# Gate and up products of eight blocks: two of eight pairs of k tiles by seven block products

## The chip, the core and the metric

The kernel runs on one core of a Trainium2 chip. The metric is the device time of one execution in microseconds; the time before is the median of three runs. TensorE (PE in the profile) multiplies, VectorE (DVE), ScalarE (ACT) and GpSimd (POOL) work elementwise, SyncE (SP) issues most of the loads.

## The reference

One layer on 256 tokens of width 2048: a first gated feed-forward network (FFN) of width 5632, a mixer (an RWKV-7 scan and a pooling branch), and a second FFN, each between two norms and added to the residual. All is fp32. The change touches the two FFNs:

```python
def _swiglu(x, w_gate, w_up, w_down):
    return (jax.nn.silu(x @ w_gate) * (x @ w_up)) @ w_down

f = _swiglu(_rmsnorm(h, ln_ffn1_pre[l]), ffn1_gate[l], ffn1_up[l], ffn1_down[l])
h = h + MACARON_WEIGHT * _rmsnorm(f, ln_ffn1_post[l])
```

## The kernel before

Every fp32 product is made of three matmuls: each operand is split into a rounded high part H and a rest L, and H·H, H·L and L·H are added up in PSUM (`mm3`). For weights the split is done on the way: SyncE loads a tile of two k tiles by 512 columns (512 KB, buffer `w32`, 4 of them), ScalarE casts it to `wH`, VectorE subtracts to get `wL` (`two`; 5 buffers each of `wH` and `wL`). So each weight tile passes SyncE, ScalarE, VectorE and TensorE in turn. A buffer is free again when its last reader is done: a `w32` after `wL` is made, a `wH` and `wL` after the tile's last matmul.

`ffn` works through 11 blocks of 512 hidden columns. In a block `gemm_tok` makes the gate product, 16 k tiles by two halves h of 128 tokens, into two PSUM banks, then the up product. The norm of the input isn't applied to the inputs `uT` but to the products: `ev_g` and `ev_u` multiply by the row factor `rs[h]`, a scalar of each token. `ev_g` makes silu, `ev_u` multiplies and turns the block in 32 by 32 pieces into `T1` (`turn`, VectorE). `shuffle_split` then puts the pieces in place with 16 ScalarE copies of 32 partitions each into `x32`, casts them to H (ScalarE) and subtracts (VectorE): two of the tiles `hT` that the down product reads. It was called at the end of the block it belongs to.

The down product is made by `post` and `seven`, two column ranges of 512 at once. There six pairs of k tiles (`NQ`) are taken out of the plain sum: the pair of k tiles, the two token halves and the two column ranges make a 2 by 2 by 2 product of blocks, and `quad` makes it with seven block products in place of eight (Winograd's form). It needs sums of inputs (`sums`: `sx`, four `sf`, `sH`, `sL`; one call serves two quads) and sums of weights: `t13` and `t24`, made by VectorE from two `w32` buffers loaded by four 256 KB transfers. A quad splits 3.5 weight tiles where two plain pairs split 2. The products go to eight PSUM banks, and `merge` and `finish` add them up. In which place of the sequence of pairs a quad stands is listed in `QUADS`.

In which order the instructions stand in each engine's queue is decided when the program is built, by a scheduler that keeps its own estimate of times; code under `high_priority` (weight splits, evictions) goes ahead of other code. Only the beginnings and ends of the products with `lead` and `trail` are ordered by hand. Each engine then works its queue strictly in order: an instruction that waits holds up all behind it.

Lines that the prediction's steps name: 134 and 135 (cast and subtraction of a weight tile), 158 to 160 (the three matmuls), 218 to 231 (`sums`), 279 to 294 (`quad`: loads, `t13`, `t24`, splits), 322 to 331 (`merge`, `finish`), 466 (transposes), 483 (`turn`), 493 to 497 (`shuffle_split`), 512 to 518 (gate and up evictions).

Of the kernel before, what the change touches and what calls it, by code (L numbers as in the profile page):

```python
# [54 lines left out]
class Block:  # L55
    def __init__(s, tc, ctx):
        s.tc = tc
        s.nc = nc = tc.nc
        E = ctx.enter_context
        s.n = 0  # L60
        s.late, s.after, s.items, s.events, s.now = [], [], deque(), [], 0.0
        s.cp = E(tc.tile_pool(name="cp", bufs=1))
# [99 lines left out]
    def gemm_tok(s, w, c0, at, KT, evac, lead=False, trail=False, xs=None):  # L162
# [71 lines left out]

    def seven(s, w, cf, cl, at, KT, T, sm, ev_first, ev_last, trail):


        nc = s.nc
        V = nc.vector
        n = NQ  # L240
        K0 = 2 * n
# [18 lines left out]
        ws = {}  # L260

        def keep(tiles):
            ws.update((k, (wH, wL)) for k, wH, wL in tiles)

        def pair(k, c0, b):
            keep(s.load_w(w, k, 2, c0, 512))
            for i in range(2):
                for h in range(2):
                    mul(f"{b}{h}", rows(k + i, h), ws[k + i])

        def quad(q):
            k = 2 * q
            if len(sm) < min(q + 2, n):
                s.sums(T, sm)
            va, vb = [s.wp.tile([P, 1024], F32, tag="w32", name=s.nm("w32"), bufs=W32_BUFS)
                      .rearrange("p (a c) -> p a c", a=2) for _ in range(2)]
            for dst, kk, c0 in ((va[:, 0], k, cl), (vb[:, 0], k, cf), (va[:, 1], k + 1, cf),
                                (vb[:, 1], k + 1, cl)):
                nc.sync.dma_start(out=dst, in_=w[kk * P:kk * P + P, c0:c0 + 512])
# [40 lines left out]
        def merge():  # L320
            with s.tc.high_priority(offset=BOOST):
                nc.scalar.copy(u[0], bank["p1"])
                for o, b, i in ((1, "p6", 0), (2, "p7", 1), (3, "p5", 2), (1, "p5", 1),
                                (1, "f0", 1), (3, "f1", 3)):
                    V.tensor_tensor(out=u[o], in0=bank[b], in1=u[i], op=ALU.add)
                ev_first(0, u[1])
                ev_first(1, u[3])

# [4 lines left out]
        for i, k in enumerate(tiles):  # L333
            pair(k, cl, "l")
            if i in QUADS[trail][1]:
# [8 lines left out]
        s.now = 0.0  # L344
        s.by_half(w, cl, stop, KT, 0.0, AHEAD[0],
                  lambda k, h: mul(f"l{h}", rows(k, h), ws[k]), keep, finish)
# [155 lines left out]
    def ffn(s, wg, wu, wd, uT, rs, gpost, resid, emit, reload, xs=None):  # L502
        nc = s.nc
        hT = s.new_T(NKF // 4)
        at = s.T_at(uT)
        for b in range(NKF // 4):
            sig = [None, None]
# [9 lines left out]
            def ev_u(h, ps):  # L517
# [10 lines left out]
        s.post(wd, s.T_at(hT), NKF, gpost, 0.5, resid, emit, reload, hT)  # L528

    def post(s, wd, at, KT, gpost, fac, resid, emit, reload, hT=None):  # L530
        nc = s.nc
# [51 lines left out]
        if hT:  # L583
            sm = []
            for c in (0, 2):
                s.seven(wd, c * 512, c * 512 + 512, at, KT, hT, sm, ev_of(c), ev_of(c + 1),
                        c == 2)
            return
# [98 lines left out]
    def mixer(s, prm, uT, rs, resid, emit, gpost, reload):  # L687
# [13 lines left out]

        for h in range(2):
            t = s.tmp("rb")
            nc.vector.tensor_copy(t[:, :P], rs[h].to_broadcast([P, P]))
            ps = s.psum("rb")
            nc.tensor.transpose(ps[:, :P], t[:, :P], s.ident)
            nc.scalar.copy(s.rsb[:, h * P:h * P + P], ps[:, :P])

# [645 lines left out]
```

## Time and profile before

| | |
|---|---|
| median of 3 runs | 2091.64 us (2089.87 to 2092.41) |
| the profiled execution | 2090.64 us, of which the span from the first to the last instruction is 2088.9 us |
| TensorE's mean granted clock | 0.998 of full speed |
| TensorE, VectorE, ScalarE busy in one gate/up block of 43.52 us | 43.52, 24.34, 25.11 us |
| the same in 175 us of the first down product | 175.00, 143.39, 94.92 us |
| HBM | 194 GB/s over the span |

How to read the rows that follow. In the order of time a row is: start, duration, engine, line, operation, what it writes and reads, how many, and in brackets how long the engine idled before it and for whom. In the table by stretches it is: the stretch, its length, then the busy time of TensorE's matmuls, its weight loads, VectorE, ScalarE and GpSimd with the number of instructions, the granted TensorE clock, the share of the DMA engines and GB/s. In the groups by line it is: line, engine, operation, shapes, count, then busy us and mean ns, then idle us before and its releaser. A row of waits is: who waited for whom, us in total, times, longest. Matmuls are pipelined: they start about 0.227 us apart and each lasts 0.39 us in the records.

### The profile page before, as it was taken

Reading aid. Unit: us, or ns where it says so; the run is one execution under the profiler, and the core shown is the slowest. Engines: PE = TensorE matmul, PEld = TensorE weight load, DVE = VectorE, ACT = ScalarE, POOL = GpSimd, SP = SyncE. Lnnn points to the kernel's source line nnn. Section 1 sums busy time; section 2 is a strip of 40 time slices with the busy share of each in tenths; the row PEclk is TensorE's granted clock in tenths of the full one; section 3 lists DMA queues with packets and bytes.
Section 4 is the critical chain, followed back from the end, with each engine's and each line's share of the span. In section 5 each row is a group of like instructions: output and inputs, shape, how many; then the busy total and the mean of one; then the engine's idle time right before and its main releaser. Section 6 shows DMA issues by size and latency. Waiting matters only on the chain.

```text
span 2088.9 us, 29095 instructions
## 1 busy us (share of the span) xinstructions
PE 2072.3 (99%) x11017; PEld 1745.5 (84%) x11017; DVE 1387.7 (66%) x1776; ACT 1156.1 (55%) x1658; POOL 76.0 (4%) x161
## 2 busy tenths in 40 slices
PE   9999999999999999999999999999999999999998
PEld 7888888887888899999888788888888888878886
DVE  6555555556887765799688666575555555568876
ACT  6565555655555565474465444466655566555543
POOL 0000000000000010000110110010000000000000
PEclk9999999999999999999999999999999999999999
DMA  7656666565767766656456565566566666646674
GB/s 256 194 176 211 193 194 194 176 211 154 226 200 252 219 190 187 178 166 193 132 159 193 157 247 190 197 219 192 182 202 196 196 192 181 203 162 220 201 242 161
DMA packets 224885, 406.99 MB, mean 195 GB/s; under 512 B 13919, under 2 KB 49897, under 8 KB 224745
## 3 DMA queue, kind: packets, MB, share of 16 engines
q1 hardware_dynamic: 218569, 384.69, 59.8%
q0 software_dynamic: 5888, 19.93, 2.7%
q8 instruction: 86, 1.41, 0.3%
q10 hardware_dynamic: 288, 0.52, 0.1%
q14 instruction: 54, 0.44, 0.1%
HBM read 396.69 MB, written 8.39 MB: 194 GB/s over the span
## 4 chain that ended last, share of the span: by engine, by line
PE 95%; DVE 2%; issue 2%; ACT 1%; POOL 0%; DMA 0%; POOLq 0%; DVEq 0%; ACTq 0%
PE mm L158 26%; PE mm L159 26%; PE mm L160 26%; PE mc L438 10%; PE ms L159 1%; PE ms L160 1%; PE ms L158 1%; PE tr L466 1%; ACT x L493 1%; PE pA L1075 0%; DVE wL L135 0%; DVE wL L294 0%; PE pSa L1183 0%; DMA x<-in_x_dram 0%; DVE sx L218 0%
## 5 line engine op out<-in xcount | busy, mean ns | idle before, releaser
L135 DVE TENSOR_TENSOR wL<-w,wH 128x1024 fp32r<-128x1024 f32 (+2 forms) x677 | 810.6, 1209 | 552.2 <-ACT wH L134 549.0
L134 ACT CAST wH<-w 128x1024 fp32r<-128x1024 f32 (+2 forms) x677 | 698.0, 1044 | 625.5 <-PE mm L160 464.9
L159 PE MATMUL mm<-wL,xH 128*128 128x512 f32 x2316 | 902.2, 390 | 0.5 <-DVE wL L135 0.5
L160 PE MATMUL mm<-wH,xL 128*128 128x512 f32 x2316 | 902.2, 390 | 0.0
L158 PE MATMUL mm<-wH,xH 128*128 128x512 f32 x2316 | 896.5, 391 | 0.0
L160 PEld LDWEIGHTS mm<-wH,xL 128*128 128x128 f32 x2316 | 435.0, 188 | 91.6 <-DVE xL L474 0.8
L158 PEld LDWEIGHTS mm<-wH,xH 128*128 128x128 f32 x2316 | 435.2, 188 | 90.3
L159 PEld LDWEIGHTS mm<-wL,xH 128*128 128x128 f32 x2316 | 435.3, 188 | 89.9 <-DVE wL L135 1.3
L438 PE MATMUL mc<-xH,wH 128*128 128x256 f32 x560 | 159.5, 285 | 0.0
L438 PE MATMUL mc<-xL,wH 128*128 128x256 f32 x560 | 158.4, 283 | 0.0
L438 PE MATMUL mc<-xH,wL 128*128 128x256 f32 x560 | 158.3, 283 | 0.0
L493 ACT COPY x<-T 32x256 f32<-32x256 f32 x352 | 141.9, 403 | 3.9
L438 PEld LDWEIGHTS mc<-xH,wH 128*128 128x128 f32 x560 | 106.0, 189 | 1.1
L438 PEld LDWEIGHTS mc<-xH,wL 128*128 128x128 f32 x560 | 106.0, 189 | 0.2
L438 PEld LDWEIGHTS mc<-xL,wH 128*128 128x128 f32 x560 | 106.0, 189 | 0.1
L293 ACT CAST wH<-t 128x1024 fp32r<-128x1024 f32 x48 | 50.5, 1053 | 64.2 <-DVE t L286 47.9
L293 ACT CAST wH<-w 128x1024 fp32r<-128x1024 f32 (+1 forms) x48 | 40.0, 838 | 58.8 <-DMA w<-in_ffn_down_dram 48.3
L294 DVE TENSOR_TENSOR wL<-t,wH 128x1024 fp32r<-128x1024 f32 x48 | 58.6, 1221 | 20.9 <-ACT wH L293 20.8
L547 POOL DMA_DIRECT2D gb<-in_ln_ffn_post_dram x4 | 2.4, 592 | 1215.1 <-DVE wL L294 1215.1
L283 DVE TENSOR_TENSOR t<-w,w 128x1024 f32<-128x1024 f32 x24 | 29.4, 1224 | 23.7 <-DMA w<-in_ffn_down_dram 22.1
L294 DVE TENSOR_TENSOR wL<-w,wH 128x1024 fp32r<-128x1024 f32 (+1 forms) x48 | 44.2, 952 | 0.7 <-ACT wH L293 0.6
L512 ACT ACTIVATE sg<-mm,rs 128x512 f32<-128x512 f32 x44 | 29.9, 689 | 22.3 <-PE mm L160 22.3
(284 smaller groups left out, 1502.9 us busy)
## 6 DMA issues: line engine op xcount, KB each, us to landing
w<-in_ffn_up_dram SPq DMA_DIRECT2D x176, 512.0 KB
w<-in_ffn_gate_dram SPq DMA_DIRECT2D x174, 512.0 KB
w<-in_ffn_down_dram SPq DMA_DIRECT2D x128, 512.0 KB
w<-in_w_in_dram SPq DMA_DIRECT2D x128, 512.0 KB
w<-in_ffn_down_dram SPq DMA_DIRECT2D x96, 256.0 KB
w<-in_w_out_dram SPq DMA_DIRECT2D x32, 512.0 KB
w<-in_w_proj_b_dram SPq DMA_DIRECT2D x16, 512.0 KB
w<-in_w_proj_a_dram SPq DMA_DIRECT2D x16, 512.0 KB
```

Of the source, the lines that this page charges most:

```text
L134: s.nc.scalar.copy(vH, v)
L135: s.nc.vector.tensor_tensor(out=vL, in0=v, in1=vH.bitcast(F32), op=ALU.subtract)
L158: nc.tensor.matmul(ps, aH, bH, start=start, stop=False)
L159: nc.tensor.matmul(ps, aH, bL, start=False, stop=False)
L160: nc.tensor.matmul(ps, aL, bH, start=False, stop=stop)
L283: V.tensor_tensor(out=t13, in0=va, in1=vb[:, :1].to_broadcast([P, 2, 512]), op=ALU.subtract)
L293: nc.scalar.copy(H, v)
L294: V.tensor_tensor(out=L, in0=v, in1=H.bitcast(F32), op=ALU.subtract)
L438: s.nc.tensor.matmul(o, lh, rh, start=one and n == 0, stop=k == KT - 1 and n == 2, skip_group_check=True)
L466: nc.tensor.transpose(ps[:, i], src[:, i * P:(i + 1) * P], s.ident)
L493: nc.scalar.copy(dst[q * 32:q * 32 + 32, :, :, i], src[i * 32:i * 32 + 32, :, :, q])
L512: nc.scalar.activation(out=sg, in_=ps, func=AF.Sigmoid, scale=rs[h])
```

## The change

Blocks 2 to 9 of each FFN (`FAST`) make the gate and up product in one call of `seven`: the gate's 512 columns are its first range, the up's 512 its second, and two pairs of k tiles (k 0 to 3) are quads. The first quad stands after the fourth pair of the gate (of six), the second after the second pair of the up product. The sums of inputs must hold the normed input, so `normed` builds it once per FFN at the end of block 0: `spread` lays the row factor out along the free axis (two transposes), and each of four `uT` tiles is put together, multiplied by it, and split again into `nT` (three VectorE operations and one cast each). One call of `sums` on `nT` serves all eight blocks. Blocks 0 and 1 are made as before, block 10 as before but on `nT` with a factor of 1.

In the new evictions `ev_f` lets ScalarE write the sigmoid into a PSUM bank that is free (`p1` or `p6`) and multiplies, `ev_l` multiplies and turns.

The carrying of a block's `T1` into `hT` (the 16 copies and the split) is put off: it is entered into the list `soft`, and `soften` empties it in the middle of the next product (in `gemm_tok` at k tile 8, in `seven` at its fifth pair). The tiles of `hT` are made then and not at the beginning. The first sum for the down product is made in block 10 between gate and up, and later ones two pairs after a quad, in place of ahead of it.

```diff
+FAST = range(2, 10)
@@ gemm_tok
             for k2 in range(k0, k1, 4):
+                if k2 == 8:
+                    s.soften()
@@
-    def seven(s, w, cf, cl, at, KT, T, sm, ev_first, ev_last, trail):
+    def seven(s, wf, cf, wl, cl, at, KT, T, sm, n, spots, ev_first, ev_last, trail=False):
...
-        n = NQ
         K0 = 2 * n
...
-        def pair(k, c0, b):
+        def pair(k, w, c0, b):
             keep(s.load_w(w, k, 2, c0, 512))
+            since[0] += 1
+            if since[0] == 2 and len(sm) == n - left["p1"] < n:
+                s.sums(T, sm)
...
         def quad(q):
             k = 2 * q
-            if len(sm) < min(q + 2, n):
-                s.sums(T, sm)
...
             mul("l1", rows(k + 1, 1), t4)
-
-        if not sm:
-            s.sums(T, sm)
+            since[0] = 0
+
...
         for i, k in enumerate(range(K0, KT, 2)):
-            pair(k, cf, "f")
-            if i in QUADS[trail][0]:
+            pair(k, wf, cf, "f")
+            if i == 4:
+                s.soften()
+            if i in spots[0]:
                 quad(next(q))
...
-                ev_first(0, u[1])
-                ev_first(1, u[3])
+                ev_first(0, u[1], bank["p1"])
+                ev_first(1, u[3], bank["p6"])
@@ ffn
-        hT = s.new_T(NKF // 4)
+        hT, sm = [], []
...
+        def carry(T1, b):
+            hT.extend(s.new_T(1))
+            s.shuffle_split(T1, hT, b)
...
-                    s.shuffle_split(T1, hT, b)
-
+                    s.soft.append(lambda T1=T1, b=b: carry(T1, b))
+
+            def ev_f(h, u, free):
+                nc.scalar.activation(out=free, in_=u, func=AF.Sigmoid)
+                nc.vector.tensor_tensor(out=u, in0=u, in1=free, op=ALU.mult)
+                sig[h] = u
+
+            def ev_l(h, o):
+                nc.vector.tensor_tensor(out=o, in0=o, in1=sig[h], op=ALU.mult)
+                s.turn(T1, h, o)
+                if h == 1:
+                    s.soft.append(lambda T1=T1, b=b: carry(T1, b))
+
+            if b in FAST:
+                s.seven(wg, b * 512, wu, b * 512, s.T_at(nT), NKD, nT, su, 2, ((3,), (1,)),
+                        ev_f, ev_l)
+                continue
+            if b > 1:
+                rs = [1.0, 1.0]
+                at = s.T_at(nT)
             s.gemm_tok(wg, b * 512, at, NKD, ev_g, lead=(b == 0), xs=xs if b == 0 else None)
+            if b == nb - 1:
+                s.sums(hT, sm)
             s.gemm_tok(wu, b * 512, at, NKD, ev_u)
             while s.after:
                 s.after.pop(0)()
+            if b == 0:
+                nT, su = s.normed(uT, rs), []
+                s.sums(nT, su)
...
+    def spread(s, rs, out):
+
+        for h in range(2):
+            t = s.tmp("rb")
+            s.nc.vector.tensor_copy(t[:, :P], rs[h].to_broadcast([P, P]))
+            ps = s.psum("rb")
+            s.nc.tensor.transpose(ps[:, :P], t[:, :P], s.ident)
+            s.nc.scalar.copy(out[:, h * P:h * P + P], ps[:, :P])
+
+    def normed(s, uT, rs):
...
+        for (uH, uL), (nH, nL) in zip(uT, nT):
+            x = s.unit((P, 4, S), F32, "nx")
+            V.tensor_tensor(out=fl(x), in0=fl(uH).bitcast(F32), in1=fl(uL).bitcast(F32),
+                            op=ALU.add)
+            V.tensor_tensor(out=x, in0=x, in1=rb.unsqueeze(1).to_broadcast([P, 4, S]),
+                            op=ALU.mult)
+            nc.scalar.copy(fl(nH), fl(x))
+            V.tensor_tensor(out=fl(nL), in0=fl(x), in1=fl(nH).bitcast(F32), op=ALU.subtract)
+        return nT
+
+    def soften(s):
+        while s.soft:
+            s.soft.pop(0)()
```

In the mixer the code that laid out the row factor is replaced by a call of `spread`, with the same instructions.

More of the change, by code (lines that the diff above doesn't have):

```diff
@@ L61, in __init__ @@
         s.late, s.after, s.items, s.events, s.now = [], [], deque(), [], 0.0
+        s.soft = []
         s.cp = E(tc.tile_pool(name="cp", bufs=1))
@@ L260, in seven @@
         ws = {}
+        since = [0]
         def keep(tiles):
             ws.update((k, (wH, wL)) for k, wH, wL in tiles)
-        def pair(k, c0, b):
+        def pair(k, w, c0, b):
             keep(s.load_w(w, k, 2, c0, 512))
+            since[0] += 1
+            if since[0] == 2 and len(sm) == n - left["p1"] < n:
+                s.sums(T, sm)
             for i in range(2):
@@ L272, in quad @@
             k = 2 * q
-            if len(sm) < min(q + 2, n):
-                s.sums(T, sm)
             va, vb = [s.wp.tile([P, 1024], F32, tag="w32", name=s.nm("w32"), bufs=W32_BUFS)
                       .rearrange("p (a c) -> p a c", a=2) for _ in range(2)]
-            for dst, kk, c0 in ((va[:, 0], k, cl), (vb[:, 0], k, cf), (va[:, 1], k + 1, cf),
-                                (vb[:, 1], k + 1, cl)):
+            for dst, kk, w, c0 in ((va[:, 0], k, wl, cl), (vb[:, 0], k, wf, cf),
+                                   (va[:, 1], k + 1, wf, cf), (vb[:, 1], k + 1, wl, cl)):
                 nc.sync.dma_start(out=dst, in_=w[kk * P:kk * P + P, c0:c0 + 512])
@@ L333, in seven @@
         for i, k in enumerate(tiles):
-            pair(k, cl, "l")
-            if i in QUADS[trail][1]:
+            pair(k, wl, cl, "l")
+            if i in spots[1]:
                 quad(next(q))
@@ L503, in ffn @@
         nc = s.nc
-        hT = s.new_T(NKF // 4)
+        hT, sm = [], []
         at = s.T_at(uT)
-        for b in range(NKF // 4):
+        nb = NKF // 4
+        def carry(T1, b):
+            hT.extend(s.new_T(1))
+            s.shuffle_split(T1, hT, b)
+        for b in range(nb):
             sig = [None, None]
@@ L527, in ffn, with post @@
                 s.after.pop(0)()
-        s.post(wd, s.T_at(hT), NKF, gpost, 0.5, resid, emit, reload, hT)
-    def post(s, wd, at, KT, gpost, fac, resid, emit, reload, hT=None):
+            if b == 0:
+                nT, su = s.normed(uT, rs), []
+                s.sums(nT, su)
+        s.post(wd, s.T_at(hT), NKF, gpost, 0.5, resid, emit, reload, hT, sm)
+    def spread(s, rs, out):
[6 more added lines that the diff above has]
+    def normed(s, uT, rs):
+        nc = s.nc
+        V = nc.vector
+        rb = s.rtmp("rsb")
+        s.spread(rs, rb)
+        nT = s.new_T(len(uT))
+        fl = lambda t: t.rearrange("p k t -> p (k t)")
+        for (uH, uL), (nH, nL) in zip(uT, nT):
[10 more added lines that the diff above has]
+            s.soft.pop(0)()
+    def post(s, wd, at, KT, gpost, fac, resid, emit, reload, hT=None, sm=None):
         nc = s.nc
@@ L583, in post @@
         if hT:
-            sm = []
             for c in (0, 2):
-                s.seven(wd, c * 512, c * 512 + 512, at, KT, hT, sm, ev_of(c), ev_of(c + 1),
-                        c == 2)
+                ev = ev_of(c)
+                s.seven(wd, c * 512, wd, c * 512 + 512, at, KT, hT, sm, NQ, QUADS[c == 2],
+                        lambda h, u, _: ev(h, u), ev_of(c + 1), c == 2)
             return
@@ L700, in mixer @@
         s.gemm_tok(w_in, GB, at, NKD, ev_sig(lambda h: sgb0[:, h]), lead=True)
[L702 to L707, printed above, removed]
+        s.spread(rs, s.rsb)
         s.R = [s.unit(p="R") for _ in range(15)]
```

2 lines of the change are left out of this document (1 added, 1 removed).

## The prediction

> **What bounds the kernel now.** I read the page first (busy shares, chain of waits), then TensorE's own waits, then one gate/up block in order of time on VectorE and ScalarE, then the first quad of the down product, which is the shape that the change brings into the gate/up stage.
>
> ```profile
> span 2088.9 us, 29095 instructions
> PE 2072.3 (99%) x11017; PEld 1745.5 (84%) x11017; DVE 1387.7 (66%) x1776; ACT 1156.1 (55%) x1658; POOL 76.0 (4%) x161
> PE 95%; DVE 2%; issue 2%; ACT 1%; POOL 0%; DMA 0%; POOLq 0%; DVEq 0%; ACTq 0%
> ...
> PE ms L158 <- ACT wH L293: 3.8, 4, 1.7
> PE warm L363 <- POOL ident masks.py:199: 1.7, 1, 1.7
> ```
>
> TensorE is busy for 99% of the span and carries 95% of the chain; of its waits the largest, 3.8 us in four pieces, stands in the down products, on the ScalarE cast of a quad. So a matmul fewer is worth its full pitch, and a microsecond by which a weight tile is late is lost in full.
>
> ```profile
> 295.20 1.43 DVE L513 SCALAR_TENSOR_TENSOR sg<-mm,rs,sg 128x512 f32<-128x512 f32 x2 [0.45 <-ACT sg L512]
> 304.40 1.23 DVE L135 TENSOR_TENSOR wL<-w,wH 128x1024 fp32r<-128x1024 f32 x1 [1.50 <-ACT wH L134]
> 317.74 0.70 DVE L483 STREAM_TRANSPOSE T<-sg 128x512 f32<-128x512 f32 x1
> 318.37 1.18 DVE L135 TENSOR_TENSOR wL<-w,wH 128x1024 fp32r<-128x1024 f32 x1
> 328.32 2.36 DVE L135 TENSOR_TENSOR wL<-w,wH 128x1024 fp32r<-128x1024 f32 x2 [6.38 <-ACT wH L134]
> 338.72 1.43 DVE L513 SCALAR_TENSOR_TENSOR sg<-mm,rs,sg 128x512 f32<-128x512 f32 x2 [0.45 <-ACT sg L512]
> ...
> 303.31 1.05 ACT L134 CAST wH<-w 128x1024 fp32r<-128x1024 f32 x1 [1.67 <-PE mm L160]
> 320.59 6.63 ACT L493 COPY x<-T 32x256 f32<-32x256 f32 x16
> 327.24 2.00 ACT L134 CAST wH<-w 128x1024 fp32r<-128x1024 f32 x2
> ...
> 295.20:338.72 43.52, 43.52 (x194) 36.05 (x193) 24.34 (x24) 25.11 (x36) 0.00 (x0) 1.00 0.64 194
> ```
>
> One block: 43.52 us from gate eviction to gate eviction, 192 matmuls, so **0.2267 us a matmul** and 2.72 us for a pair of k tiles (12 matmuls). TensorE is busy throughout (43.52 of 43.52). Casts go out when TensorE frees a buffer (1.67 us idle each, then 1.05 us; VectorE starts its wL 0.04 us after). The 16 shuffle copies hold ScalarE for 6.63 us, and VectorE idles 6.38 us behind them. It costs nothing today: five weight buffers are up to 13.6 us of matmuls.
>
> **The change, part by part.** *Matmuls removed.* A quad replaces eight block products by seven, three matmuls each; two quads, eight blocks, two FFNs: 96 matmuls, 96 × 0.2267 = **−21.8 us**. Two 128x128 transposes per FFN are added in `spread`:
>
> ```profile
> 735.06 1.31 PE tr L466 x12
> ```
>
> 0.11 us each, **+0.4 us**. A fast block then has 186 matmuls, 42.2 us.
>
> *VectorE's added work.* From the groups by line:
>
> ```profile
> L293 ACT CAST wH<-t 128x1024 fp32r<-128x1024 f32 x48 | 50.5, 1053 | 64.2 <-DVE t L286 47.9 <-PE mm L160 10.2 <-DVE t L283 5.6
> L283 DVE TENSOR_TENSOR t<-w,w 128x1024 f32<-128x1024 f32 x24 | 29.4, 1224 | 23.7 <-DMA w<-in_ffn_down_dram 22.1 <-issue 1.4
> L286 DVE TENSOR_TENSOR t<-w,t 128x512 f32<-128x512 f32 x24 | 16.5, 686 | 0.2
> L325 DVE TENSOR_TENSOR u<-ms,u 128x512 f32<-128x512 f32 x16 | 10.6, 683 | 0.0
> ```
>
> Per fast block: 12 pair wL, 2 × (three wL and t13) and one xL, 21 ops of 1.22; 2 × (one half wL and two t24 halves), six merge adds, two finishes, four eviction multiplies and two turns, 20 of 0.69: 39.4 us busy, against 24.34 now. Back to back they follow each other at 1.14 and 0.60 us (318.37 less 317.74 gives 0.63 for a turn; 2.36 us for two wL gives 1.14), so 36.2 of 42.2 us. VectorE alone does not become the bound, but its order decides.
>
> *The order at the first quad.* The changed program's queues are known before it runs. In each of seven blocks per FFN (blocks 3 to 9) ScalarE's stands so (A1 to A4 are the quad's four splits: va, b21, t13, t24; F5 the next pair):
>
> ```
> cast A1   after the last matmul of the block before (buffer, five back)
> cast A2   after the block's first pair, F1
> cast A3   after VectorE's t13
> 16 copies of the block before's T1, after VectorE's second turn
> cast A4, cast F5
> ```
>
> VectorE's: finish ×2, wL A1, multiply ×2, wL A2, turn, t13, turn, t24, wL A3, t24, wL A4, wL F5. Let 0 be the end of the last matmul of the block before.
> - A1's cast runs 0.03 to 1.08. F1 and two matmuls hoisted before its end release A2's buffer at 3.2; cast 0.6; wL A2 at 3.9; turn at 4.5; t13 5.1 to 6.3.
> - cast A3 from 6.4; next op 0.95 later, at 7.4 (two casts in 2.00 us); 16 copies, 6.63: 14.0; cast A4: 15.1. TensorE has it at 15.15.
> - TensorE begins F1 at −0.16 (matmuls start 0.227 apart and last 0.39), and before A4 stand F1 to F4 (48), A1 (6), A2 (3), A3 (6): 63 × 0.2267 − 0.16 = 14.1.
>
> So TensorE **waits 1.0 us** for A4's wH. Behind it stand two matmuls on A4, then two on F5's wH, whose cast follows A4's by 0.95 us: 16.1 against 15.6, 0.5 us more, and 0.1 for F5's wL. Together 1.6 us in a block that saves 6 × 0.2267 = 1.36. The wait comes again each block, since A1's cast starts from the block's end: 14 × 1.6 = **+22.4 us**. Ends: 0 if the copies end 1.0 us earlier (in the row above a train of 16 costs TensorE nothing); above, 2.1, ten steps off by 0.05 us. I take 1.6, by the rows of just these operations. The second quad (B) has no copies before its last cast. Its t13 waits for weights whose buffers F5 and F6 free at 17.4 and 18.6:
>
> ```profile
> 565.07 0.96 SPq L279 DMA_DIRECT2D w<-in_ffn_down_dram  x2
> 568.30 1.23 DVE L283 TENSOR_TENSOR t<-w,w 128x1024 f32<-128x1024 f32 x1 [0.76 <-DMA w<-in_ffn_down_dram]
> ```
>
> 3.2 us after issue, so t13 of B is at 21.9 and B4's wL ready at 29.6, 2.4 us before TensorE wants it: nothing.
>
> *Block 2.* There the shuffles of blocks 0 and 1 are both due. In FFN1 ScalarE runs cast A1, cast sH, 10 copies, cast A2, 6 copies, cast xH, then A3, which waits for a t13 that stands behind xL: 2.0 + 16 × 0.414 (6.63 by 16) + 0.6 + 1.0 = 10.2, xL 1.1, turns 1.3, t13 1.2: 13.9; A3 to 14.9; 14 copies, 5.8; A4 ready at 21.7 where TensorE wanted 14.1. With F5's 0.5 that is 8.2 us. In FFN2 16 copies stand earlier, before F4's cast, and 16 again before A4: F4 2.6, A1 3.5, xH 4.5, t13 8.5, A3 9.6, copies to 16.2, A4 17.3: 3.8 us. **+12.0 us**, ends 8 and 16 (a third either way, for the longer chain).
>
> *Clock.*
>
> ```profile
> 514.00:520.00 6.00, 4.10 (x17) 2.74 (x16) 6.00 (x9) 4.57 (x5) 0.00 (x0) 1.00 0.53 166
> 520.00:526.00 6.00, 5.75 (x26) 4.43 (x24) 6.00 (x7) 3.36 (x4) 0.00 (x0) 1.00 0.67 207
> ...
> 2078.00:2082.00 4.00, 1.74 (x8) 1.12 (x6) 1.38 (x3) 0.72 (x2) 0.39 (x1) 1.00 0.00 0
> 2082.00:2086.00 4.00, 0.00 (x0) 0.00 (x0) 2.87 (x5) 0.00 (x0) 0.53 (x1) 0.58 0.46 168
> ```
>
> The 1.9 us lost at 514 to 520 left the granted clock at 1.00; after the last matmul it is 0.58 from about 4 us of idling on. FFN1's block 2 waits 4.6 us in one piece: 0, or 4 us at 0.58, 1.7 us lost; I take the middle, **+0.9 us**. [...]
>
> *Sums moved.* The first two rows above are the start of FFN1's down product: 1.90 + 0.25 us lost where VectorE is full (6.00 of 6.00), with the sums, xL and the quad together. FFN2's:
>
> ```profile
> 1866.00:1872.00 6.00, 4.10 (x17) 2.79 (x16) 5.97 (x8) 2.47 (x3) 0.00 (x0) 1.00 0.25 88
> 1872.00:1878.00 6.00, 5.78 (x25) 4.39 (x24) 6.00 (x8) 4.59 (x5) 0.00 (x0) 1.00 0.53 175
> ```
>
> The first sum now lies in block 10, and eight pairs precede the first quad: wL and shuffle end near 13 us, the quad's last wL at 20.7, TensorE wants its first at 21.6. **−4.3 us**; 0 if another wait fills the place.
>
> *`normed`, first sums.* 17.5 us of VectorE per FFN (12 ops at 1.14 and the sums' 3.8) in blocks 0 and 1, which leave 43.52 − 24.34 = 19.2 us idle, less 1.2 for an xL now put off: hidden. Without that cover, at most the 2.1 us of the down start twice. A copied T1 waits for no DMA, and the DMA bytes per block are the same; the merge's waits (on p6) stand behind three wL already done: 0.
>
> Sum: −21.8 + 0.4 + 22.4 + 12.0 + 0.9 − 4.3 = **+9.6 us**. The profiled execution took 2090.64 us, 1.7 beyond its span, and lies 1.0 below the median of 2091.64. 2090.6 + 9.6 = 2100.2, at the median **2101 us**.
>
> **The rivals.**
> - *TensorE stays the only bound (faster).* The place is cast A4. If it is ready by 14.1 us after the block's end, 1.0 us sooner than my chain, no wait is left in 14 blocks. With block 2 hidden too: 2091.6 − 21.4 − 4.3 = 2066 us. For it: the train of 16 costs nothing today. Against it: today's train meets buffers full of pairs, and here a quad of 21 matmuls with t13, turn and train in series. [...]
> - *Same mechanism, waits a fifth to a third smaller (no change).* 34.4 us of waits become 24 to 28: 2091 to 2095.
> - *Quad B waits too (slower).* The 2.4 us of lead is lost if its transfers land 3.4 us later, as the 512 KB loads at higher load might; 16 × 1 us more: 2117.
> - *The sums' move gains nothing*: 2105, inside the forecast.
>
> **How the numbers follow.** Forecast 0.55 (its own range 2096 to 2108), no change 0.20, only bound TensorE 0.13, quad B 0.12. Within 0.2%, 4.2 us, is what a measurement of this kernel can tell from no change. Faster 0.13, same 0.20, slower 0.55 + 0.12 = 0.67. The ends of the unknown costs give waits of 14 × 1.1 + 8 = 23 to 14 × 2.1 + 16 = 45 us, so 2089 to 2111 from the 2066 of the first rival; I take 2085 to 2116, toward the rivals on both sides.
>
> **What would show it.** TensorE waits on ScalarE's quad cast, some 1.0 us (and 0.5 on the next pair), once in each fast block; ScalarE's 16 copies between its third and fourth quad cast; blocks 43.5 to 43.9 us apart, not 42.2; in FFN1 one wait near 4.6 us with the clock under 1.00; no loss at the first quad of the down product. A copy train ended before 14.1 us, or blocks 42.2 us apart, would make it wrong.

## The result, and the profile after

| | us |
|---|---|
| before, median of its runs | 2091.64 (2089.87 to 2092.41) |
| changed kernel, median of four runs | **2118.09** (2115.17 to 2121.94) |
| ratio | **1.0129**, 95% interval 1.0115 to 1.0143 |
| profiled execution of the changed kernel | 2117.5, span 2115.8 |

Slower, as forecast, but by 26.5 us (1.3%) where the sum gave 9.6, and 2 us above the range. The page of the changed kernel (span, busy shares, chain of waits by engine) and TensorE's waits (us in total, times, longest) answer to the lines shown of before:

```profile
span 2115.8 us, 29577 instructions
PE 2068.7 (98%) x10925; PEld 1729.3 (82%) x10925; DVE 1613.3 (76%) x2104; ACT 1214.4 (57%) x1752; POOL 76.0 (4%) x161
PE 72%; DVE 10%; ACT 7%; issue 6%; DMA 5%; POOL 0%; SPq 0%; ACTq 0%; DVEq 0%; POOLq 0%
```

```profile
PE ms L160 <- ACT wH L298: 29.8, 18, 3.4
PE mm L160 <- ACT wH L136: 2.8, 13, 0.2
```

TensorE has 92 matmuls fewer (96 removed, 4 added) and yet the span is 26.9 us longer: its wait on the quads' cast went from 3.8 us in 4 pieces to 29.8 in 18, and a short wait on the next pair follows 13 times. The chain, 95% TensorE before, now runs through VectorE, ScalarE and the loads as well. A stop costs more than its idle time, since a matmul's record lasts 0.39 us and the next could start 0.227 after it. So from here on a *wait* is what the starts of successive matmuls are apart beyond 0.227 us, summed over one stop; matmuls that start 0.427 us apart under a halved clock are counted by themselves, 0.20 each.

The block that begins at 239.3 us, first ScalarE, then VectorE, then TensorE, in order of time (start, duration, instruction, idle time before it and its releaser):

```profile
239.38 1.06 ACT L298 CAST wH<-w 128x1024 fp32r<-128x1024 f32 x1 [1.17 <-PE mm L162]
242.55 0.62 ACT L298 CAST wH<-w 128x512 fp32r<-128x512 f32 x1 [2.12 <-PE mm L162]
246.08 1.06 ACT L298 CAST wH<-t 128x1024 fp32r<-128x1024 f32 x1 [2.91 <-DVE t L288]
247.04 6.63 ACT L499 COPY x<-T 32x256 f32<-32x256 f32 x16
253.69 1.04 ACT L298 CAST wH<-t 128x1024 fp32r<-128x1024 f32 x1
...
238.29 1.22 DVE L137 TENSOR_TENSOR wL<-w,wH 128x1024 fp32r<-128x1024 f32 x1
239.43 0.68 DVE L538 TENSOR_TENSOR u<-u,ms 128x512 f32<-128x512 f32 x1
240.03 1.28 DVE L337 TENSOR_TENSOR u<-mm,u 128x512 f32<-128x512 f32 x2
241.23 1.21 DVE L299 TENSOR_TENSOR wL<-w,wH 128x1024 fp32r<-128x1024 f32 x1
242.36 1.28 DVE L542 TENSOR_TENSOR u<-u,u 128x512 f32<-128x512 f32 x2
243.56 0.68 DVE L299 TENSOR_TENSOR wL<-w,wH 128x512 fp32r<-128x512 f32 x1
244.16 0.70 DVE L489 STREAM_TRANSPOSE T<-u 128x512 f32<-128x512 f32 x1
244.79 1.18 DVE L288 TENSOR_TENSOR t<-w,w 128x1024 f32<-128x1024 f32 x1
...
254.79 0.50 PE L160 MATMUL ms<-wH,sH 128*128 128x512 f32 x1 [1.21 <-ACT wH L298]
```

The order is the forecast's, operation by operation: casts A1, A2, A3, the train of sixteen copies, then A4, and TensorE stopped for A4. What differs is the clock time of one step. The two finishing adds (L337) begin 0.73 us after the block's end, behind the last up pair's wL and a multiply (L538) of the block before, and from there VectorE runs without a gap: two adds, wL A1, two multiplies, wL A2 at 4.3, turn, t13 at 5.5. The forecast had wL A2 at 3.9, bound by A2's cast, and t13 at 5.1. A4's cast ends at 15.4.

The time between blocks is read from the first quad casts (A1) of blocks 3 and 9, first FFN and second:

```profile
151.43 1.05 ACT L298 CAST wH<-w 128x1024 fp32r<-128x1024 f32 x1 [1.66 <-PE mm L162]
416.17 1.05 ACT L298 CAST wH<-w 128x1024 fp32r<-128x1024 f32 x1
...
1514.17 1.06 ACT L298 CAST wH<-w 128x1024 fp32r<-128x1024 f32 x1 [0.73 <-ACT ms L537]
1786.03 1.06 ACT L298 CAST wH<-w 128x1024 fp32r<-128x1024 f32 x1 [1.02 <-PE mm L162]
```

Six blocks in 264.7 us and in 271.9 us are 44.1 and 45.3 us a block, against 42.2 without waits and 43.8 forecast.

The second difference is the clock. These windows (TensorE, weight loads, VectorE, ScalarE, GpSimd busy, then granted clock, DMA share, GB/s) are 3.41 us wide:

```profile
429.71:433.12 3.41, 0.96 (x4) 0.50 (x4) 0.32 (x1) 3.34 (x7) 0.00 (x0) 1.00 0.26 101
433.12:436.53 3.41, 3.41 (x9) 2.19 (x8) 3.41 (x4) 3.41 (x5) 0.00 (x0) 0.50 0.09 10
...
1709.69:1713.11 3.42, 1.86 (x7) 1.25 (x8) 2.10 (x2) 3.40 (x5) 0.00 (x0) 1.00 0.00 0
1713.11:1716.52 3.41, 3.41 (x17) 2.65 (x16) 3.41 (x4) 2.62 (x3) 0.00 (x0) 1.00 0.52 169
...
1754.07:1757.48 3.41, 1.63 (x7) 1.05 (x7) 1.86 (x2) 3.37 (x6) 0.00 (x0) 1.00 0.00 1
1757.48:1760.89 3.41, 3.41 (x10) 2.63 (x9) 3.41 (x4) 2.85 (x4) 0.00 (x0) 0.50 0.56 159
```

In these rows, behind a window in which TensorE was busy for 1.63 us or less the next runs at 0.50, with 9 or 10 matmuls touched instead of 17; behind one with 1.86 us or more it runs at 1.00. Seven such windows at half clock lie in the trace: three in the first FFN's block 2 (115.68 to 125.92), one in its block 9, and three in the second FFN. The four that stand alone last 3.41 us each, the three in block 2 together 10.24. Stops of 2.3 us (from 1753.7) to 3.9 us (from 1480.8) were enough.

Where the 26.9 us lie, from the starts of the matmuls:

| term | forecast | trace after |
|---|---|---|
| matmuls removed, transposes added | −21.4 | −21.4 |
| waits in the 14 blocks 3 to 9 | +22.4 | +32.1 |
| half clock behind them | 0 | +4.0 |
| waits in the two blocks 2 | +12.0 | +12.0 (8.0 and 3.9) |
| half clock in blocks 2 | +0.9 | +3.3 (2.3 and 1.0) |
| waits in the two down products | −4.3 | −3.9 (5.9 before, 2.0 after) |
| sum | +9.6 | +26.1 |

The last 0.8 us are in no term. The 5.9 us of waits before stand at the starts of the two down products (514 and 1869 us); after, none is left there, and the 2.0 us stand deeper in (0.6 at 591 and 1.4 at 2052 us).

### The profile page after: what moved, and what is told of

The parts are those of the page before. It is cut to its first block, busy times and chain, and to the rows that moved or that the text cites. A ratio compares the mean times of both kernels' runs of the same rounds, so it can differ in the third digit from the quotient of the medians.

```text
span 2115.8 us, 29577 instructions
## 1 busy us (share of the span) xinstructions
PE 2068.7 (98%) x10925; PEld 1729.3 (82%) x10925; DVE 1613.3 (76%) x2104; ACT 1214.4 (57%) x1752; POOL 76.0 (4%) x161
## 4 chain that ended last, share of the span: by engine, by line
PE 72%; DVE 10%; ACT 7%; issue 6%; DMA 5%; POOL 0%; SPq 0%; ACTq 0%; DVEq 0%; POOLq 0%
PE mm L160 19%; PE mm L162 18%; PE mm L161 18%; PE mc L444 10%; ACT x L499 3%; DMA w<-in_ffn_gate_dram 3%; DVE wL L137 3%; DVE wL L299 2%; ACT wH L298 2%; DMA w<-in_ffn_down_dram 1%; ACT wH L136 1%; PE ms L161 1%; PE ms L162 1%; PE ms L160 1%; DVE u L331 1%
## 5 line engine op out<-in xcount | busy, mean ns | idle before, releaser
L137 DVE TENSOR_TENSOR wL<-w,wH 128x1024 fp32r<-128x1024 f32 (+2 forms) x613 | 730.0, 1207 | 226.7 <-ACT wH L136 223.4
L136 ACT CAST wH<-w 128x1024 fp32r<-128x1024 f32 (+2 forms) x613 | 627.6, 1042 | 406.9 <-PE mm L162 206.7
L161 PE MATMUL mm<-wL,xH 128*128 128x512 f32 x2124 | 830.2, 391 | 0.0
L162 PE MATMUL mm<-wH,xL 128*128 128x512 f32 x2124 | 827.2, 391 | 0.7 <-DVE xL L480 0.7
L160 PE MATMUL mm<-wH,xH 128*128 128x512 f32 x2124 | 808.5, 394 | 2.8 <-ACT wH L136 2.8
L299 DVE TENSOR_TENSOR wL<-t,wH 128x1024 fp32r<-128x1024 f32 x112 | 136.7, 1222 | 126.0 <-ACT wH L298 125.7
L298 ACT CAST wH<-t 128x1024 fp32r<-128x1024 f32 x112 | 117.4, 1050 | 155.0 <-DVE t L291 81.4
L298 ACT CAST wH<-w 128x1024 fp32r<-128x1024 f32 x112 | 93.6, 837 | 165.5 <-DMA w<-in_ffn_down_dram 69.6
L299 DVE TENSOR_TENSOR wL<-w,wH 128x1024 fp32r<-128x1024 f32 x112 | 104.2, 951 | 6.7 <-ACT wH L298 6.6
L160 PE MATMUL ms<-wH,sH 128*128 128x512 f32 x168 | 65.2, 404 | 29.8 <-ACT wH L298 29.8
L161 PE MATMUL ms<-wL,sH 128*128 128x512 f32 x168 | 67.2, 400 | 1.6 <-DVE wL L299 1.6
```

What stands on the lines that cost most here:

```text
L136: s.nc.scalar.copy(vH, v)
L137: s.nc.vector.tensor_tensor(out=vL, in0=v, in1=vH.bitcast(F32), op=ALU.subtract)
L160: nc.tensor.matmul(ps, aH, bH, start=start, stop=False)
L161: nc.tensor.matmul(ps, aH, bL, start=False, stop=False)
L162: nc.tensor.matmul(ps, aL, bH, start=False, stop=stop)
L298: nc.scalar.copy(H, v)
```

## The experiments

Each run was timed beside runs of the kernel before on the same chip, whose medians there lay between 2090.4 and 2091.8 us. The rival that has most to be said for it is VectorE: it gains some 12 us of busy time per block (24.34 us of 43.52 before, 36.62 of 42.00 in e1 below), its share rises from 66 to 76%, and a reader of the busy shares would blame it.

**e1: the train shortened.**

```diff
-        for i in range(4):
-            for q in range(4):
-                nc.scalar.copy(dst[q * 32:q * 32 + 32, :, :, i],
-                               src[i * 32:i * 32 + 32, :, :, q])
+        nc.scalar.copy(x32.rearrange("p k t -> p (k t)"), T1)
```

> The sixteen 32x256 shuffle copies of each carried block are replaced by one 128x1024 copy of T1; the placing of the 32x32 blocks is left out, everything else stays. Theory (the train of copies ahead of the last cast of the first quad makes the wait): that cast starts some 8.5 us after the block's end instead of 14.5, so the waits of the fourteen blocks 3 to 9 (32.1 us, and 4.0 us of half clock behind them) and of both blocks 2 (12.0 and 3.3) go, with the 2.0 us left in the down products: 2118 - 53 = 2065 us, blocks 42.2 us apart, clock 1.00 throughout. Rival one (VectorE's chain of multiply, finish, turn and t13 is what is late, the copies only fill the time): half or more of the waits stay: 2090 us or above. Rival two (the weight loads are late): the waits move to the next pairs: 2100 us or above.

Measured: **2064.84 us** (2063.89 to 2067.43), ratio 0.9874 (0.9857 to 0.989). The page's busy shares, and a window one block long:

```profile
PE 2048.7 (99%) x10925; PEld 1726.3 (84%) x10925; DVE 1620.3 (79%) x2104; ACT 1105.4 (54%) x1422; POOL 76.0 (4%) x161
```

```profile
236.00:278.00 42.00, 42.00 (x187) 34.79 (x186) 36.62 (x42) 23.29 (x25) 0.00 (x0) 1.00 0.63 201
```

VectorE does all that it did, 36.62 us of 42, and TensorE is busy for 42.00 of 42.00. All the waits, the half clock and both blocks 2 hang on 330 small copies, by which ScalarE was busy for 109 us of its 1214; VectorE's load alone costs nothing. Its place in the chain was still to be shown.

**e2: the train moved into the second quad.**

```diff
-            if i == 4:
+            if i == 4 and n > 2:
                 s.soften()
...
             pair(k, wl, cl, "l")
+            if i == 3 and not trail and n == 2:
+                s.soften()
             if i in spots[1]:
```

> The carried block's copies are called after the fourth up pair; in ScalarE's queue fifteen of them then stand between the second and the third cast of the second quad, none in the first. Theory: the first quad no longer waits (-36 us in blocks 3 to 9), and the wait follows the train: the third cast of the second quad, 263.66 in the block at 239 us, goes out 6.2 us later where TensorE has about 2 us in hand: some 4 us in each of 14 blocks (+56 us), and since each is longer than the waits that halved the clock before, half clock behind most of them (14 times 1.0 to 1.7 us): 2118 - 36 + 56 + 14 to 24 = about 2150 us (2135 to 2165). Rival one (VectorE's chain after the block's end makes the first quad late): the first quad still waits 1 us or more per block. Rival three (ScalarE has room enough there): 2070 to 2085 us.

Measured: **2110.77 us** (2105.74 to 2115.18), ratio 1.009 (1.0072 to 1.0107); its profiled execution was its fastest run. The wait did follow the train: in the trace the first quad runs through, and the second stops for the cast behind the train in 12 of the 14 blocks 3 to 9. But it is 1.8 us a block, not 4, with 4.3 us of half clock in all, and the time is 24 us below the range expected. The size was misread from the trace: the third cast of the second quad ended at 264.7 where TensorE wanted it at 268.4, so it had 3.7 us in hand, not 2, and 6.2 less 3.7 is 2.5; the other 0.7 us is not explained.

**e3: everything but the quads.**

```diff
-FAST = range(2, 10)
+FAST = ()
```

> No block goes through the quads; the scaled inputs, the input sums moved to block 10 and the carrying put off to the next block's middle stay. Theory (these parts cost nothing and the moved sums take away the 5.9 us lost at the start of the two down products): 2091.6 + 0.4 - 4.3 to -5.5 = 2087 us (2086 to 2089). Rival (the scaled inputs and the put off copies cost something too, up to 4 us, hidden in the change's total): 2090 to 2095.

Measured: **2085.59 us** (2084.53 to 2087.16), ratio 0.9971 (0.9959 to 0.9983): 6 us faster than before, and 0.4 below the range expected. The scaled inputs and the carrying put off cost nothing that shows, and with the moved sums what stood at the down products is gone: in the trace 0.5 us of waits is left in them of 5.9.

**e4: block 2 the old way.**

```diff
-FAST = range(2, 10)
+FAST = range(3, 10)
```

> Block 2 goes the old way, on the scaled inputs; blocks 3 to 9 stay fast. Theory (block 2 is late because two blocks' copies are due there): its 10.4 us in the first FFN and 4.9 us in the second go, 12 matmuls (2.7 us) come back, blocks 3 to 9 wait as before: 2118 - 15.3 + 2.7 = 2105.5 us (2103 to 2108), and no half clock near 116 us. Rival (whichever block is first fast pays, since the second input sum is made in it): block 3 takes over 5 us or more and the time is 2111 or above.

Measured: **2092.48 us** (2088.94 to 2096.51), ratio 1.0005 (0.9996 to 1.0014): 13 us below the expectation, on the side away from the rival. No half clock is left in blocks 3 to 9 (that is 4.0 us), blocks 4 to 9 wait 1.85 us each instead of 2.37 (6.3 us), and block 3, now the first fast one, does not wait at all (3.7 us in the two FFNs). Block 3 shows why; ScalarE, then VectorE, around the block's end at 144.5:

```profile
144.53 1.05 ACT L298 CAST wH<-w 128x1024 fp32r<-128x1024 f32 x1 [1.67 <-PE mm L162]
147.25 0.62 ACT L298 CAST wH<-w 128x512 fp32r<-128x512 f32 x1 [1.67 <-PE mm L162]
147.78 6.63 ACT L499 COPY x<-T 32x256 f32<-32x256 f32 x16
154.44 2.00 ACT L298 CAST wH<-t 128x1024 fp32r<-128x1024 f32 x2
...
144.04 1.28 DVE L530 SCALAR_TENSOR_TENSOR sg<-mm,sg 128x512 f32<-128x512 f32 x2
145.24 0.70 DVE L489 STREAM_TRANSPOSE T<-sg 128x512 f32<-128x512 f32 x1
```

The train is the same 6.63 us, but it begins at 3.3 and not at 7.7, for behind an ordinary block there are no finishing adds and no multiplies ahead of the turns: the turn is at 0.7 instead of 4.9. A3 and A4 then go out together and are ready at 11.9. So the train makes the wait together with the time at which VectorE lets it start.

**e8: VectorE's string shortened at the block's end.**

```diff
             def ev_f(h, u, free):
                 nc.scalar.activation(out=free, in_=u, func=AF.Sigmoid)
-                nc.vector.tensor_tensor(out=u, in0=u, in1=free, op=ALU.mult)
                 sig[h] = u
```

> The changed kernel with fast blocks 2 to 9, without the two VectorE multiplies by the sigmoid in each fast block (the gate's sigmoid is still computed and its factor left out). They stand ahead of the finishing adds at the block's end; in the changed kernel's trace the first add begins 1.05 us after the block's end on the mean, from 0.1 before to 2.0 after, and the wait is 1.3 us plus that delay. Theory: without them the adds begin at the block's end as the prediction had it: waits of 1.3 us, 14 times 1.0 us less and no half clock in blocks 3 to 9: 2118 - 14 - 4 = 2100 us (2096 to 2104). Rival (the adds are late for another reason, such as the sigmoid or TensorE's last matmul): 2112 or above.

Measured: **2093.73 us** (2091.69 to 2097.72), ratio 1.0013 (1.0004 to 1.0022): 24 us below the changed kernel, 6 more than expected and 2 below the range. With 1.2 us of VectorE's 36 per block taken away just there, the waits of blocks 3 to 9 fall from 32.1 to 13.4 us and their half clock is gone, while blocks 2 lose what they lost (11.8 us of waits and 3.0 of clock). Rows of the same block, whose end is at 237.0:

```profile
236.64 1.28 DVE L337 TENSOR_TENSOR u<-mm,u 128x512 f32<-128x512 f32 x2
...
240.80 1.18 DVE L288 TENSOR_TENSOR t<-w,w 128x1024 f32<-128x1024 f32 x1
241.91 0.68 DVE L299 TENSOR_TENSOR wL<-w,wH 128x512 fp32r<-128x512 f32 x1
```

The adds begin 0.4 us before the block's end; t13 is at 3.8, A4's cast ends at 14.2, and 0.7 us of wait is left in seven of the fourteen blocks, up to 2.0 where VectorE is late for other reasons. Not all of the gain is that of the multiplies: wL A2 (241.91) now stands behind t13, where in the changed kernel it stood ahead of it, and that brings t13 forward by 0.6 us more than the shorter string does. Both act through the same step, the time of t13.

**e5: the train behind the first quad.**

```diff
+                s.last = wH
                 return [(H[:, i], L[:, i]) for i in range(m)]
...
+        if s.last is not None:
+            nc.scalar.copy(dst[:, 0, 0, :, 0], s.last[:, :4].bitcast(F32))
         for i in range(4):
             for q in range(4):
```

> Blocks 3 to 9 fast, and the train can no longer stand ahead of the first quad's last cast: its destination is first touched by a ScalarE copy of 128x4 elements that reads that cast's wH, so the sixteen copies come behind it, between the casts of the first up pairs and the second quad's first. Theory: the 24.4 us of waits in e4's trace go but for some 1.5 us at the down products, and nothing takes their place, since the second quad has some 2.5 us in hand: 2092.5 - 23 = 2069.5 us (2067 to 2074), blocks 42.2 us apart, no half clock. Rival one (VectorE is late by itself at the block's start, the train only shows it): 1 us or more per block stays: 2080 or above. Rival two (the train's wait follows it to the second quad, as in e2_train_in_B where 1.9 us per block came back): 2092 or above.

Measured: **2099.97 us** (2095.6 to 2100.9), ratio 1.0039 (1.0025 to 1.0053): rival two. Each of the 14 blocks waits 1.1 to 2.8 us, in the second quad, or in the two blocks 3 on a pair just ahead of it. ScalarE, VectorE and TensorE in one block:

```profile
379.20 6.63 ACT L504 COPY x<-T 32x256 f32<-32x256 f32 x16
385.85 1.57 ACT L300 CAST wH<-w 128x1024 fp32r<-128x1024 f32 x2
387.33 1.05 ACT L507 CAST xH<-x 128x1024 fp32r<-128x1024 f32 x1
391.12 1.05 ACT L300 CAST wH<-t 128x1024 fp32r<-128x1024 f32 x1 [2.75 <-DVE t L290]
...
386.93 1.83 DVE L301 TENSOR_TENSOR wL<-w,wH 128x1024 fp32r<-128x1024 f32 x2 [6.28 <-ACT wH L300]
388.68 1.22 DVE L508 TENSOR_TENSOR xL<-x,xH 128x1024 fp32r<-128x1024 f32 x1
389.81 1.22 DVE L290 TENSOR_TENSOR t<-w,w 128x1024 f32<-128x1024 f32 x1
...
392.22 0.73 PE L160 MATMUL ms<-wH,sH 128*128 128x512 f32 x2 [0.83 <-ACT wH L300]
```

Here the train holds not one cast but four steps: B1's and B2's casts stand behind it, VectorE idles 6.28 us for their wL, and the quad's t13 stands behind these and behind the carried block's xL, which waits for an xH that is behind the train too. t13 itself reads only the loaded weights.

**e6 and e7: the first quad later.** e6 puts it behind the sixth gate pair, e7 behind the fifth (`((4,), (1,))`, with the copies called where they were):

```diff
-FAST = range(2, 10)
+FAST = range(3, 10)
...
-            if i == 4:
+            if i == 4 and n > 2 or i == 1 and n == 2:
                 s.soften()
...
-                s.seven(wg, b * 512, wu, b * 512, s.T_at(nT), NKD, nT, su, 2, ((3,), (1,)),
+                s.seven(wg, b * 512, wu, b * 512, s.T_at(nT), NKD, nT, su, 2, ((5,), (1,)),
```

> Blocks 3 to 9 fast, the first quad behind the sixth gate pair rather than the fourth; no other work moves by hand, and the copies stand between the quad's first casts. Theory: TensorE wants the quad's last weights 5.4 us later after the block's end, at 19.6 us, where the train's own time is unchanged (it ends near 14 us): no wait at the first quad. 2092.5 - 23 = 2069.5 us (2067 to 2074). Rival one (the second quad now follows too close and its transfers land late, for the weight buffers are freed by the first quad's casts): 1 to 2 us per block in the second quad: 2080 to 2095. Rival two (VectorE's load as such): 2085 or above.

> As e6_A_behind_F6 with the first quad behind the fifth gate pair: TensorE wants its last weights 2.7 us later than in e4_fast_from_3, where the last cast ended 1.7 us too late on the mean. In ScalarE's queue the train and the carried block's cast now stand ahead of the third cast of the quad, so the third and fourth cast end near 15.5 and 16.5 us where TensorE wants them near 15.5 and 16.8. Theory: 0 to 0.5 us of wait per block: 2068 to 2076 us. Rival (VectorE's load): 2085 or above.

Measured: e6 **2112.11 us** (2110.32 to 2112.51), ratio 1.0095 (1.008 to 1.011); e7 **2120.7 us** (2116.61 to 2121.63), ratio 1.0134 (1.0119 to 1.0149). Both are more than 35 us above the theory, and by the times alone the rival with VectorE's load would stand. The first quad stops for some 3 us in 12 of the 14 blocks (2.4 to 2.9 in e6, with 9.0 us of half clock; 3.0 to 4.9 in e7). ScalarE and VectorE in e6:

```profile
284.90 6.63 ACT L499 COPY x<-T 32x256 f32<-32x256 f32 x16
291.57 1.05 ACT L502 CAST xH<-x 128x1024 fp32r<-128x1024 f32 x1
295.10 1.04 ACT L298 CAST wH<-t 128x1024 fp32r<-128x1024 f32 x1 [2.48 <-DVE t L288]
...
292.65 1.23 DVE L503 TENSOR_TENSOR xL<-x,xH 128x1024 fp32r<-128x1024 f32 x1 [6.35 <-ACT xH L502]
293.80 1.22 DVE L288 TENSOR_TENSOR t<-w,w 128x1024 f32<-128x1024 f32 x1
```

The same knot as in e5: t13 stands behind xL, xL behind xH, xH behind the train. VectorE idles 6.35 us with t13 next but one, which is not what an engine with too much work does. The later place also moved xL ahead of t13 in the queue, which neither expectation had looked at. (The quad's weights were there: the casts A1 and A2 of the same two tiles stand ahead of the train.) VectorE didn't take t13 ahead of xL: it starts at 293.80, straight behind.

**e9 and e10: the same, with xH held back.** The cast xH gets something to wait for, so that xL falls behind the quad (e9 behind F6, e10 behind F5 with `i == 4`):

```diff
-            if i == 4:
+            if i == 4 and n > 2:
                 s.soften()
             if i in spots[0]:
                 quad(next(q))
+            if i == 5 and n == 2:
+                s.soften()
...
         dH, dL = T[j]
+        if s.last is not None:
+            nc.scalar.copy(dH[:, 0, :4], s.last[:, :4])
         nc.scalar.copy(dH, x32)
```

> As e6_A_behind_F6 (blocks 3 to 9 fast, first quad behind the sixth gate pair), and the cast xH of the carried block is held back until the first quad's fourth cast, by a ScalarE copy of 128x4 elements into xH that reads that cast's wH. In VectorE's queue the first quad's t13 and t24 then stand ahead of the carried block's xL; in e6's trace t13 stood behind that xL, xL behind xH and xH behind the train (VectorE idle 6.35 us there). Theory (in-order queues: the wait is the train plus what stands behind it, and goes if nothing of the quad does but its third and fourth casts): the train runs from about 6.5 to 13.2 us after the block's end, the fourth cast ends near 15.2 us where TensorE wants it near 19.6: no wait in the first quad, none in the second: 2092.5 - 23 = 2069.5 us (2066 to 2074), no half clock. Rival (VectorE's load, 21 operations of 1.14 us and 20 of 0.60 in 42.2 us, is the cause whatever the order): 2085 or above.

> The same with the first quad behind the fifth gate pair. In ScalarE's queue the train stands between the third and the fourth cast, as in the changed kernel, but TensorE wants the fourth 2.7 us later. Theory: third cast from 7.8 us after the block's end, train to 15.4, fourth cast to 16.4 where TensorE wants it near 16.8; where VectorE's finishing adds are late by more than half a microsecond a wait of that excess stays: 0 to 0.8 us in each of 12 blocks: 2070 to 2079 us. Rival (VectorE's load): 2085 or above.

Measured: e9 **2071.22 us** (2070.54 to 2072.73), ratio **0.9904** (0.989 to 0.9919); e10 **2077.61 us** (2077.26 to 2078.01), ratio 0.9934 (0.9918 to 0.9951). e9 is e6 with xH and xL behind the quad's work, not ahead of it, and 41 us faster with the same load on VectorE. The copies are called at another place too, but their train stands where it stood: 7.4 us ahead of the first quad's first matmul in both (284.90 and 292.33 in e6, 278.40 and 285.79 in e9). VectorE and ScalarE in one block of e9, whose predecessor ends at 269.6:

```profile
271.58 1.28 DVE L342 TENSOR_TENSOR u<-mm,u 128x512 f32<-128x512 f32 x2
...
276.94 1.18 DVE L290 TENSOR_TENSOR t<-w,w 128x1024 f32<-128x1024 f32 x1
...
278.40 6.64 ACT L504 COPY x<-T 32x256 f32<-32x256 f32 x16
285.06 2.00 ACT L300 CAST wH<-t 128x1024 fp32r<-128x1024 f32 x2
...
287.31 1.06 ACT L509 CAST xH<-x 128x1024 fp32r<-128x1024 f32 x1
```

t13 is done before the train begins, both casts follow the train at once, and TensorE takes these weights at 287.83 without a stop. VectorE is as late here as in the worst blocks of the changed kernel (the adds begin 1.9 us after the end of the block before), and the train runs from 8.8 to 15.4 us after it, not from 6.5 to 13.2 as the theory had it; it costs nothing, since the casts behind it end at 17.4. The waits in the two FFNs from 50 us into the span on are 5.9 us together, and no block runs at half clock. This version beats both kernels: it is 20 us below the kernel before on its chip. e10 has the shorter time in hand that the theory gave it: 0.4 to 1.7 us of wait in most blocks, and a time within the range expected.

**e11: block 2 in that version.** `FAST = range(2, 10)` again.

> As e9_A_behind_F6_xL_late with block 2 fast as well. Theory (block 2's wait is that of two blocks' copies in one queue): 12 matmuls less (-2.7 us), and in the first FFN's block 2 ScalarE runs the sums' cast, 16 copies, three casts, the carried block's xH and, behind xL, two turns and t13, the third cast to about 16.7 us after the block's end, 14 more copies, 5.8 us, and the fourth cast to 23.5, where TensorE wants it near 19.6: a wait of 3.9 us, with up to 1.7 us of half clock behind it; second FFN 0 to 2 us. 2071.2 - 2.7 + 3.9 + 0 to 3.7 = 2072 to 2076, in the trace one wait near 4 us about 118 us into the span. Rival (the late place of the quad covers block 2 as it does the others): 2068.5, no such wait.

Measured: **2077.62 us** (2075.7 to 2078.32), ratio 0.9936 (0.9923 to 0.995). TensorE's waits in the trace:

```profile
PE ms L160 <- ACT wH L300: 4.1, 1, 4.1
```

One stop of 4.1 us, forecast 3.9, at 118.7 us into the span, and two windows of half clock behind it. The time is 1.6 us above the range expected. Two blocks' copies in one queue do not fit ahead of one quad.

**e12: the sums put back.** In e9, the down product's input sums are made where they were before.

> As e9_A_behind_F6_xL_late with the down product's input sums where the kernel before had them: the first at the start of its first pair of columns, each next one ahead of the quad before. Theory (the moved sums took away what VectorE lost there): the waits at the start of the two down products, 2.96 and 2.95 us in the kernel before's trace against 1.26 and 0.3 in e9's, come back: 2071.2 + 4.3 = 2075.5 us (2074 to 2077). Rival (the waits went since fewer operations stand in block 10 and the sums' place does not count): 2071 us, unchanged within 1.5.

Measured: **2074.58 us** (2073.97 to 2079.87), ratio 0.9928 (0.9915 to 0.994); 3.4 us above e9. Waits of 2.0 us come back at the start of each down product (507.6 and 1854.9 us). By these medians the move is worth 3.4 us here. The slowest of these runs is the profiled one; it has a window at half clock in the last down product that adds to it.

## Why the prediction was wrong in its size

- *What bounds, and matmuls removed:* right. e1 reaches 2065 with the same matmuls, where the first rival, TensorE alone, had 2066.
- *VectorE's added work:* right that its load is no bound (e1, 87% busy). But "36.2 of 42.2 us" (21 × 1.14 and 20 × 0.60 are 35.9; measured 36.62 of 42.00) is a mean over the block, and at the block's end VectorE has no slack: in the trace after it is busy 9.00 of 9.00 us from 232 to 241.

```profile
232.00:241.00 9.00, 9.00 (x42) 7.44 (x41) 9.00 (x12) 5.29 (x6) 0.00 (x0) 1.00 0.86 277
```

- *The order at the first quad: here the first step failed.* The order was right, and that A4 stands behind the train. The sum let the finishing adds start with the block's end, so that A2's cast set wL A2 at 3.9. In the trace after they start 1.0 us after it on the mean (0.1 us before it to 2.0 after), behind work of the block before, and VectorE's string, not A2's cast, sets t13, A3, the train and A4. The wait is 1.24 us in the block where the adds are at −0.1 and 3.46 where they are at 2.0: one for one, some 1.3 us and the lateness of the adds. So 14 × 2.3 = 32.1 us, not 14 × 1.6 = 22.4; the upper end of 2.1 allowed ten steps 0.05 us off, not a string that starts late. e8 takes 1.2 us out of that string, with t13 ahead of wL A2 besides, and the waits fall to 1.0 us a block; e9 leaves the adds as late (1.1 us on the mean) and puts the quad later, and the waits go.
- *Quad B's lead of 2.4 us:* right in the changed kernel (in the block at 239.3 the last cast ends at 268.6 and its wL at 269.85; TensorE takes the one at 271.15 and the other at 271.83). No second quad stopped. In e2 and e5, with the train there, it does.
- *Block 2:* 8.0 and 3.9 us of waits where the sum had 8.2 and 3.8. In the first FFN they came in two stops, which begin at 111.4 and 116.6 us, the longest piece 3.7, not in one piece of 4.6. e4 and e11 agree that it is the copies of two blocks.
- *Clock: here the second step failed.* The sum gave 0.9 us, for one block, and nothing for the other waits. The granted clock was halved for seven windows in five places, 7.3 us. Waits grown from 1.6 to between 2.3 and 3.5 us were long enough where most of one fell into one window: of the windows of 3.41 us above, one with 1.63 us of TensorE busy was followed by half clock, one with 1.86 us was not. Nor was "about 4 us of idling" a right reading of the kernel before: there TensorE's last matmul ends at 2079.74 and the clock is halved from 2082.61 on, 2.9 us later, behind a window with 0.54 us of TensorE busy. The stretches at half clock in the trace after lie on one grid, wherever the stops began: the second to the fifth begin 93, 401, 428 and 481 times 3.413 us after the first.
- *Sums moved, normed hidden:* right in what they do (e3, e12); that −3.9 came for −4.3 is in part luck. The starts of the down products lost 5.9 us before, more than the 4.3 read from the busy times, and all of it went; 2.0 us of new waits came deeper in.
- *The rivals:* "TensorE stays the only bound" named the right place, cast A4, and the right point, 14.1 us; the runs put the kernel on the other side of it. "Quad B waits too" would have given 2117, close to the time that came, but it is not what happened.

What stays open is why VectorE's lateness at the block's end varies from block to block. Blocks 4 to 9 wait half a microsecond less when block 2 isn't stopped (e4), and their adds are that much less late, 0.6 us on the mean where the changed kernel has 1.1; why is not shown. No run was made for it.

## What to carry to other kernels

Price an operation by what stands behind it in its engine's queue, and start the string from the time that queue is really free, not from the event that it needs: a microsecond of backlog at the end of each block was worth 10 us of waits here, and a cast and a subtraction put behind the quad instead of ahead of it 41. A low busy share says nothing about a queue at the moment when it counts; read the last ten microseconds ahead of the critical step. A long train of small copies belongs where nothing with a deadline, directly or through another engine's queue, follows it.

## What the runs showed of the hardware

In the changed kernel a stop that left TensorE busy for 1.63 us or less of one 3.41 us window was followed by a window at half clock: 1.0 to 1.6 us besides the stop for each of the four that stand alone, behind stops of 2.3 to 3.9 us, and nothing for a stop of 3.0 us that fell across two windows (the row at 1709.69 holds its larger part); no window there with 1.86 us or more was followed by one. Once halved, the clock was back at 1.00 behind the first window in which TensorE was busy for all its 3.41 us, five times of five; in the first FFN's block 2 it stayed at 0.50 behind windows with 1.57 and 1.81 us. From full clock, 1.79 us was followed by half clock in e4 (5.30 to 8.72) and 1.53 us in e12 (2008.02 to 2011.44). What lies between 1.79 and 1.86 us, and whether busy time alone decides, is not shown. So here a stop of 2.3 to 3.9 us cost nothing besides itself or 1.0 to 1.6 us more, by where it fell.
